# Transposing x as it lands and making h in three parts of 2, 2 and 4 k tiles

## The chip, the cores and the metric

The kernel runs on one core of a Trainium2 chip. The metric is the device time of one execution in microseconds; the time before is the median of three runs.

PE is TensorE, DVE is VectorE, ACT is ScalarE, POOL is GpSimd, SP is SyncE, which here only issues DMAs.

## The reference, cut to what matters

One layer of a hybrid block over 512 latent tokens and 256 context tokens with 1024 channels. The change lies wholly in its beginning, the modulated norm ahead of the input projection:

```python
mod  = split(silu(c)     @ w_mod + b_mod, 6)      # c:     one row of 1024
modc = split(silu(c_ctx) @ w_mod + b_mod, 6)      # c_ctx: the context's row
h  = rmsnorm(x,   norm1_g) * (1 + mod[1])  + mod[0]
hc = rmsnorm(ctx, norm1_g) * (1 + modc[1]) + modc[0]
u  = h  @ w_in                                    # gates, q, k, v, ... of three branches
uc = hc @ w_in
# mLSTM, differential attention and SSD on u and uc; gated sum, w_out, residual;
# second modulated norm, gated conv FFN, residual
```

`rmsnorm(x, g)` is `x * rsqrt(mean(x*x) + eps) * g`, the mean over the 1024 channels of a token.

## The kernel before

Everything is float32. Products with weights are made of float32r halves: a matrix is split into a high part (a cast on ACT) and a low part (a subtraction on DVE, every third one on POOL), and a product is high x high + high x low + low x high. h is kept with the channels on the partitions, as 8 k tiles of 128 channels: `hlat[0]`, `hlat[1]` (high and low part, 128 x 8 x 512) for the latent tokens and `hctx` (128 x 8 x 256) for the context.

**Phase 0** (lines 222 to 401) makes h. `xs` holds the 768 tokens in six tiles of 128 tokens by 1024 channels, loaded by three DMAs of two tiles each, the context first. ACT squares every tile with an accumulated sum (`ssq`); `rstd` (line 124) takes the reciprocal root on DVE by Newton steps, twelve small operations in a row, once for each pair of tiles; DVE scales the pair; PE transposes it in blocks of 128 x 128 into PSUM banks `psx`, four blocks to a bank; the banks are copied to `xT` (128 x 8 x 768), by turns on ACT and DVE.

Shift and scale come from `h_part(n)` (line 333), once for each of NS = 2 halves of the channels (4 k tiles): eight DMAs of w_mod, 512 KB each, into five buffers `wm`; for each, four matmuls of 256 columns with `scl` (silu of c and c_ctx) into four row groups of one PSUM bank; a copy to `msb`, two transposes, four additions to `MT`, one operation for `A1` = (1 + scale) * norm1_g. Then for each k tile and for latent and context tokens: ACT makes h's high part from xT, A1 and MT, DVE makes the same in float32 in place, and DVE (even k) or POOL (odd k) subtracts the two to get the low part.

`early(n)` (line 367) is the share of the first projections that a part of h can feed: the gates (`wgh`, `wgl`, prepared from `wgr`), the first key columns, and two sets of query columns, four PSUM banks of results that stay open over all parts. `run` (line 150) emits the chunks of `early(n - 1)` between those of `h_part(n)`; the last part's are emitted when its h is there. Weights of the projections come through `wpiece` (line 180): two buffers `wr`, four each of `wh` and `wl`.

SP issues all these DMAs in one queue: c, c_ctx, the two pieces of wgr, ctx, the norm rows, x, w_mod with pieces of w_in between. A scheduler sets the order of each engine's instructions when the kernel is built; each engine then works them off in that order.

Behind phase 0 stand `gate_rows` (line 500), a chain of ACT and DVE operations on the result of the gates' projection, and `m_proj(0)`, further projections, whose v tiles ACT copies out of PSUM (line 645).

## Time and profile before

| | us |
|---|---|
| median of three runs | 1130.47 |
| lowest, highest | 1129.69, 1135.66 |
| the profiled execution: its span | 1133.3 |
| PE busy in the span | 1088.3 (96%) |
| DVE busy | 721.9 (64%) |
| ACT busy | 477.6 (42%) |
| POOL busy | 285.3 (25%) |

Of the profiled execution only the span is given, from its first instruction to its last; it is 2.8 us longer than the median and lies between the lowest and the highest run. PE counts as busy also where its matmuls run at the lower clock or follow each other closely, so a busy PE is not PE at its peak. Of the other engines only the time matters in which PE waits for them. A row of a timeline gives the start, the duration, the engine, the line, the operation, what it writes and reads, the count and, in brackets, the idle time before it and what ended it. `PEclk` is the granted clock: 1.00 is 2.4 GHz, 0.50 is 1.2 GHz.

### The profile page before, as it was taken

The numbers are of one execution on the slowest core, as the hardware profiler recorded it, in microseconds if no ns is written. First come the engines' busy times: TensorE is split into PE (matmuls) and PEld (weight loads), VectorE is DVE, ScalarE is ACT, GpSimd is POOL, SyncE is SP. The second block draws the span as 40 slices with busy tenths as digits, with TensorE's granted clock in tenths as the row PEclk, the third lists the DMA queues.
The fourth block names the chain that finished last, engine by engine and source line by source line (L and its number), as shares of the span: only waits on it lengthen the run. The fifth ranks groups of instructions, "written<-read, shape, count | busy, mean of one in ns | idle before, by whom it ended". The sixth has DMA issues, their size and how long they took to land.

```text
span 1133.3 us, 16687 instructions
## 1 busy us (share of the span) xinstructions
PE 1088.3 (96%) x6438; PEld 949.7 (84%) x6438; DVE 721.9 (64%) x1354; ACT 477.6 (42%) x891; POOL 285.3 (25%) x243
## 2 busy tenths in 40 slices
PE   4998999999999998999999999988999999999998
PEld 3597999988888997889998887988888888888887
DVE  6578677768645568886685567677867656651211
ACT  5455454557324233334654573333543443431110
POOL 3230001026423533551061002243212212111110
PEclk9898999999999998999999999999999999999999
DMA  8621212223334337331113202425533333333421
GB/s 297 232 59 56 71 40 57 57 70 94 112 109 117 119 108 230 91 109 54 38 38 81 74 33 79 144 63 159 152 112 93 93 100 91 107 93 93 130 93 38
DMA packets 136416, 113.00 MB, mean 100 GB/s; under 512 B 6609, under 2 KB 115512, under 8 KB 136336
## 3 DMA queue, kind: packets, MB, share of 16 engines
q1 hardware_dynamic: 135712, 111.59, 32.8%
q8 instruction: 51, 0.84, 0.3%
q0 software_dynamic: 624, 0.33, 0.2%
q14 instruction: 29, 0.24, 0.1%
HBM read 109.81 MB, written 2.10 MB: 99 GB/s over the span
## 4 chain that ended last, share of the span: by engine, by line
PE 80%; DVE 9%; DMA 3%; issue 3%; ACT 3%; POOL 2%; SPq 0%; DVEq 0%; ACTq 0%; POOLq 0%
PE pl L82 56%; PE psx L82 19%; DVE t L85 2%; PE sc L82 2%; DMA wr<-in_w_in_dram 1%; ACT t L104 1%; DVE wl L85 1%; DVE t L88 1%; DMA wm<-in_w_mod_dram 1%; PE pl L949 1%; POOL t L85 1%; ACT wh L176 1%; POOL wl L85 1%; DMA t<-in_w_mod_dram 0%; PE psx L276 0%
## 5 line engine op out<-in xcount | busy, mean ns | idle before, releaser
L85 POOL TENSOR_TENSOR wl<-wr,wh 128x1024 fp32r<-128x1024 f32 x59 | 144.5, 2450 | 629.9 <-ACT wh L176 563.4
L176 ACT CAST wh<-wr 128x1024 fp32r<-128x1024 f32 x150 | 157.9, 1053 | 292.9 <-PE pl L82 179.5
L82 PE MATMUL pl<-h,wh 128*128 128x512 f32 (+1 forms) x768 | 223.2, 375 | 4.5 <-DVE ft L88 3.0
L85 DVE TENSOR_TENSOR wl<-wr,wh 128x1024 fp32r<-128x1024 f32 x91 | 119.2, 1312 | 146.8 <-ACT wh L176 144.6
L82 PE MATMUL pl<-hl,wh 128*128 128x512 f32 x608 | 200.4, 397 | 0.6 <-ACT t L758 0.4
L82 PEld LDWEIGHTS pl<-h,wh 128*128 128x128 f32 x768 | 141.0, 189 | 31.0 <-issue 4.1
L82 PE MATMUL pl<-wh,hl 128*128 128x256 f32 x768 | 151.7, 291 | 3.2 <-ACT t L645 3.2
L82 PE MATMUL pl<-h,wl 128*128 128x512 f32 (+1 forms) x384 | 143.0, 374 | 0.0
L82 PEld LDWEIGHTS pl<-hl,wh 128*128 128x128 f32 x608 | 113.0, 189 | 24.5 <-issue 2.0
L82 PEld LDWEIGHTS pl<-wh,hl 128*128 128x128 f32 x768 | 125.2, 196 | 4.1 <-ACT t L645 3.4
L82 PE MATMUL pl<-hl,wl 128*128 128x512 f32 x304 | 120.7, 397 | 0.0
L82 PE MATMUL pl<-wl,hl 128*128 128x256 f32 x384 | 111.3, 290 | 0.0
L82 PEld LDWEIGHTS pl<-h,wl 128*128 128x128 f32 x384 | 72.6, 189 | 12.8
L82 PEld LDWEIGHTS pl<-wl,hl 128*128 128x128 f32 x384 | 75.2, 196 | 0.5
L88 DVE SCALAR_TENSOR_TENSOR ft<-pl,PT,ft 128x511 f32<-128x511 f32 x88 | 65.2, 744 | 6.1 <-ACT ft L104 4.8
L82 PEld LDWEIGHTS pl<-hl,wl 128*128 128x128 f32 x304 | 57.3, 188 | 11.4
L82 PE MATMUL psx<-wl,ah 128*128 128x512 f32 (+1 forms) x176 | 66.2, 376 | 0.0
L82 PE MATMUL psx<-wh,al 128*128 128x512 f32 (+1 forms) x176 | 66.1, 376 | 0.0
L82 PE MATMUL psx<-wh,ah 128*128 128x512 f32 (+1 forms) x176 | 66.0, 376 | 0.0
L85 DVE TENSOR_TENSOR al<-ft,ah 128x512 fp32r<-128x512 f32 x22 | 45.4, 2063 | 31.0 <-ACT ah L176 31.0
L82 PE MATMUL pl<-y,wh 128*128 128x512 f32 x192 | 61.8, 402 | 0.4 <-ACT y L104 0.3
L104 ACT ACTIVATE t<-t 128x512 f32<-128x512 f32 (+4 forms) x55 | 36.9, 684 | 35.7 <-DVE t L88 34.2
(315 smaller groups left out, 2032.2 us busy)
## 6 DMA issues: line engine op xcount, KB each, us to landing
wr<-in_w_in_dram SPq DMA_DIRECT2D x64, 512.0 KB, 4.1
wr<-in_w_up_dram SPq DMA_DIRECT2D x44, 512.0 KB, 3.8
t<-in_w_mod_dram SPq DMA_DIRECT2D x48, 256.0 KB, 4.3
wr<-in_w_down_dram SPq DMA_DIRECT2D x22, 512.0 KB, 3.7
wm<-in_w_mod_dram SPq DMA_DIRECT2D x16, 512.0 KB, 8.1
wr<-in_w_out_dram SPq DMA_DIRECT2D x8, 512.0 KB, 3.4
fc<-in_w_mod_dram SPq DMA_DIRECT2D x16, 256.0 KB, 3.0
xs<-in_x_dram SPq DMA_DIRECT2D x2, 1024.0 KB
```

The lines of the kernel that those rows point to most:

```text
L82: return PE.matmul(o, l, r, start=start, stop=stop)
L85: eng.tensor_tensor(out=o, in0=x, in1=y, op=op)
L88: V.scalar_tensor_tensor(out=o, in0=x, scalar=sc, in1=y, op0=op0, op1=op1)
L104: return S.activation(o, x, f, **kw)
L176: S.copy(hi, src)
L949: PE.transpose(out=tp[:, t * P:(t + 1) * P], in_=p0[:, (t0 + t) * P:(t0 + t + 1) * P], identity=ident)
```

## The change

- x is no longer scaled ahead of the transposes: a tile is transposed as it is when it has landed. All twelve copies of `psx` to `xT` are DVE's.
- One `rstd` for all six tiles, behind them. The six columns of reciprocal roots are spread over the channels: `dg` = identity times the root, 128 x 768, and a product of ones with it (two matmuls, 512 and 256 columns) leaves each token's root on all partitions in two PSUM banks `rsp`; ACT copies them to `rsb`.
- h is made from three steps per k tile and token set: DVE xT = xT * A1 * root (the root from PSUM in the first part, from `rsb` later), ACT high part = xT + shift, DVE low part = (xT + shift) - high part. POOL does none of it.
- The parts of the channels are 2, 2 and 4 k tiles. A part of 2 loads eight pieces of 256 KB, two to a buffer, and multiplies them two by two; 16 matmuls instead of 32, and one addition more for shift and scale each.
- wgr is loaded behind x.

```diff
-    NS, NE, EX = 2, 3, 3
+    PARTS = ((0, 2), (2, 4), (4, 8))
+    NE, EX = 3, 3
...
-        nc.sync.dma_start(wgr[:, :, 0:16], wv[:, :, C_GM:C_GM + 16])
-        nc.sync.dma_start(wgr[:, :, 16:32], wv[:, :, C_DT:C_DT + 16])
         xs = p0.tile([P, 6, D], F32, name="xs")
...
+        nc.sync.dma_start(wgr[:, :, 0:16], wv[:, :, C_GM:C_GM + 16])
+        nc.sync.dma_start(wgr[:, :, 16:32], wv[:, :, C_DT:C_DT + 16])
...
-            rstd(rs[:, 2 * i:2 * i + 2], ssq[:, 2 * i:2 * i + 2], 2, 1.0 / D)
-            for t in (2 * i, 2 * i + 1):
-                ts(V, xs[:, t, :], xs[:, t, :], rs[:, t:t + 1])
...
-                if k % 4:
-                    V.tensor_copy(o, tp.rearrange("p (k c) -> p k c", k=2))
-                else:
-                    S.copy(o, tp.rearrange("p (k c) -> p k c", k=2))
+                V.tensor_copy(xT[:, k:k + 2, i * 256:(i + 1) * 256], tp.rearrange("p (k c) -> p k c", k=2))
+        rstd(rs, ssq, 6, 1.0 / D)
+        dg = p0.tile([P, 6, P], F32, name="dg")
+        tt(V, dg, ident.unsqueeze(1).broadcast_to([P, 6, P]), rs.unsqueeze(2).broadcast_to([P, 6, P]), ALU.mult)
+        rsp = [pss(), pss()]
+        mm(rsp[0], ones.broadcast_to([P, P]), dg[:, 2:6, :].rearrange("p t c -> p (t c)"))
+        mm(rsp[1][:, 0:TC], ones.broadcast_to([P, P]), dg[:, 0:2, :].rearrange("p t c -> p (t c)"))
+        rsb = p0.tile([P, NT], F32, name="rsb")
+        S.copy(rsb[:, TC:NT], rsp[0])
+        S.copy(rsb[:, 0:TC], rsp[1][:, 0:TC])
...
+                if kw == 4 or k % 2 == 0:
+                    r = p0.tile([P, 1024], F32, tag="wm", name="wm", bufs=5)
...
+                    rv = r.rearrange("p (e s c) -> p e s c", e=2, s=2)
+                    last[0] = nc.sync.dma_start(rv[:, k % 2], wsrc)
+                    if k % 2:
+                        for q in range(4):
+                            last[1] = mm(ps[32 * q:32 * q + 32, 0:256], scl[:, k - 1 + q // 2, :], rv[:, q // 2, q % 2, :],
+                                         k == 1, k == NK - 1)
...
                 for r, cs, h_ in ((0, slice(TC, NT), hlat), (1, slice(0, TC), hctx)):
-                    hins[0] = act(h_[0][:, k, :], xT[:, k, cs], AF.Identity, scale=A1[:, k, r:r + 1], bias=MT[:, 0, k, r:r + 1])
-                    ts(V, xT[:, k, cs], xT[:, k, cs], A1[:, k, r:r + 1], MT[:, 0, k, r:r + 1], ALU.mult, ALU.add)
-                    tt(G if k % 2 else V, h_[1][:, k, :], xT[:, k, cs], h_[0][:, k, :].bitcast(F32), ALU.subtract)
+                    rb = rsb[:, cs] if n else rsp[r][:, 0:cs.stop - cs.start]
+                    stt(xT[:, k, cs], xT[:, k, cs], A1[:, k, r:r + 1], rb, ALU.mult, ALU.mult)
+                    hins[0] = act(h_[0][:, k, :], xT[:, k, cs], AF.Identity, bias=MT[:, 0, k, r:r + 1])
+                    stt(h_[1][:, k, :], xT[:, k, cs], MT[:, 0, k, r:r + 1], h_[0][:, k, :].bitcast(F32), ALU.add, ALU.subtract)
```

How the order moves on the engines is shown at three places. PE at the start, before (`crow` holds the rows of c and of the norms, `xs` x, `wm` w_mod, `msb` the copied sums):

```order
L259 MATMUL psx<-ident,crow 128x32
L276 MATMUL psx<-ident,xs 128x128 x16
L82 MATMUL pl_292<-wm,scl 32x256 x12
L276 MATMUL psx<-ident,xs 128x128 x16
L82 MATMUL pl_292<-wm,scl 32x256 x8
L276 MATMUL psx<-ident,xs 128x128 x3
L82 MATMUL pl_292<-wm,scl 32x256 x4
L276 MATMUL psx<-ident,xs 128x128 x13
L82 MATMUL pl_292<-wm,scl 32x256 x4
L325 MATMUL psx<-ident,prm 128x128
L82 MATMUL pl_292<-wm,scl 32x256 x4
L351 MATMUL psx<-ident,msb 128x128 x2
```

and now:

```order
L260 MATMUL psx<-ident,crow 128x32
L275 MATMUL psx<-ident,xs 128x128 x44
L82 MATMUL pl_269<-wm,scl 32x256 x2
L275 MATMUL psx<-ident,xs 128x128 x4
L82 MATMUL pl_269<-wm,scl 32x256 x14
L82 MATMUL psx<-dg,ones 128x512
L82 MATMUL psx<-dg,ones 128x256
L329 MATMUL psx<-ident,prm 128x128
L367 MATMUL psx<-ident,msb 128x128 x2
L82 MATMUL psx<-wm,scl 32x256 x14
L82 MATMUL pl_332<-hl_104,wgh 128x512
```

The transposes stand together ahead of nearly all modulation matmuls; the two matmuls with `dg` stand between the first part's sums and their transposes, and 14 of the second part's matmuls ahead of the first one with h.

DVE at the last part of h, before (`hl_104`, `hl_105` are the high and low part of the latent h, `hct` the context's, `A_88` is A1):

```order
L85 TENSOR_TENSOR MT<-psx,PT 128x2x2 x4
L88 SCALAR_TENSOR_TENSOR A_88<-MT,NG 128x8
L94 TENSOR_SCALAR xT<-xT,A_88,MT 128x512
L94 TENSOR_SCALAR xT<-xT,A_88,MT 128x256
L85 TENSOR_TENSOR hl_105<-xT,hl_104 128x512
L85 TENSOR_TENSOR hct<-xT,hct 128x256
```

and now:

```order
L85 TENSOR_TENSOR MT<-psx,PT 128x2x2 x4
L330 COPY PT<-psx 128x128
L88 SCALAR_TENSOR_TENSOR A_88<-MT,NG 128x8
L88 SCALAR_TENSOR_TENSOR xT<-xT,A_88,rsb 128x512
L88 SCALAR_TENSOR_TENSOR xT<-xT,A_88,rsb 128x256
L88 SCALAR_TENSOR_TENSOR xT<-xT,A_88,rsb 128x512
L88 SCALAR_TENSOR_TENSOR xT<-xT,A_88,rsb 128x256
L88 SCALAR_TENSOR_TENSOR xT<-xT,A_88,rsb 128x512
L88 SCALAR_TENSOR_TENSOR xT<-xT,A_88,rsb 128x256
L88 SCALAR_TENSOR_TENSOR xT<-xT,A_88,rsb 128x512
L88 SCALAR_TENSOR_TENSOR xT<-xT,A_88,rsb 128x256
L330 COPY PT<-psx 128x128
```

The first low part (`hl_105`) stood fifth; now it stands behind the eight products and two copies of PT. On PE, ahead of that part's first h, stood twelve matmuls of the fourth projection behind the transposes of `msb`; now the two transposes of `prm` stand there alone.

ACT behind phase 0, before (`wh<-wr` is the high part of a weight piece, `t` with `psx` or `pl` a convolution's first pass or a gate row):

```order
L176 CAST wh<-wr 128x1024
L104 ACTIVATE t_666<-psx,PT 128x512
L104 ACTIVATE t_676<-t_676 64x768
L104 ACTIVATE t_698<-psx,PT 128x512
L176 CAST wh<-wr 128x1024
L104 ACT_TABLE_LOAD
L104 ACTIVATE t_688<-t_686 64x768
L104 ACT_TABLE_LOAD
L104 ACTIVATE t_686<-t_688 64x768
L176 CAST wh<-wr 128x1024
L645 COPY t_662<-pl_803 128x128
```

and now:

```order
L104 ACTIVATE t_672<-t_672 64x768
L176 CAST wh<-wr 128x1024
L104 ACTIVATE t_662<-psx,PT 128x512
L104 ACTIVATE t_694<-psx,PT 128x512
L104 ACT_TABLE_LOAD
L104 ACTIVATE t_684<-t_682 64x768
L176 CAST wh<-wr 128x1024
L104 ACT_TABLE_LOAD
L104 ACTIVATE t_682<-t_684 64x768
L176 CAST wh<-wr 128x1024
L666 COPY t_658<-pl_799 128x128
```

A cast that stood ahead of the first of the two table loads now stands between them.

## Rows read from the trace of the kernel before

**Rows 1.** Timeline of PE: start us, duration us, operation; in brackets idle before, releaser.
```profile
8.64 0.28 PE L259 MATMUL psx<-ident,crow 32*128 32x32 f32 x1 [8.64 <-DMA crow<-in_norm_g_dram]
15.04 3.67 PE L276 MATMUL psx<-ident,xs 128*128 128x128 f32 x16 [6.12 <-DVE xs L92]
...
20.63 1.97 PE L276 MATMUL psx<-ident,xs 128*128 128x128 f32 x16
...
31.51 1.08 PE L82 MATMUL psx<-wm,scl 128*32 128x256 f32 x8 [2.62 <-DMA wm<-in_w_mod_dram]
...
54.87 0.48 PE L82 MATMUL pl<-hl,wgh 128*128 128x512 f32 x1
...
68.60 0.39 PE L82 MATMUL psx<-hl,wl 128*128 128x512 f32 x1
...
89.21 0.58 PE L82 MATMUL pl<-wh,hl 128*128 128x256 f32 x1 [3.17 <-ACT t L645]
```

**Rows 2.** Stretches: from:to, length; each engine's busy us (count); PEclk, DMA share, GB/s.
```profile
2.60:5.00 2.40, 0.00 (x0) 0.00 (x0) 0.93 (x7) 0.00 (x0) 2.39 (x7) 1.00 0.98 116
6.00:19.00 13.00, 4.24 (x21) 3.65 (x25) 7.68 (x34) 10.22 (x17) 3.85 (x8) 1.00 1.03 402
30.00:37.00 7.00, 5.49 (x30) 1.98 (x30) 7.00 (x12) 5.80 (x9) 2.38 (x2) 0.51 1.07 385
88.00:95.00 7.00, 5.79 (x27) 5.79 (x28) 6.65 (x9) 1.75 (x8) 0.00 (x0) 0.51 0.01 2
596.00:601.00 5.00, 5.00 (x27) 4.81 (x28) 4.90 (x21) 3.03 (x6) 0.00 (x0) 0.66 0.00 0
756.80:764.00 7.20, 5.71 (x45) 5.50 (x46) 7.10 (x11) 3.03 (x7) 7.09 (x5) 1.00 0.26 73
```

**Rows 3.** Timeline of ACT behind the first projections.
```profile
64.60 1.05 ACT L104 ACTIVATE t<-pl,gcol 64x512 f32<-64x512 f32 x2 [5.40 <-PE pl L82]
...
73.69 1.06 ACT L176 CAST wh<-wr 128x1024 fp32r<-128x1024 f32 x1 [1.27 <-DMA wr<-in_w_in_dram]
74.77 1.28 ACT L104 ACT_TABLE_LOAD   x1
76.06 0.84 ACT L104 ACTIVATE t<-t 64x768 f32<-64x768 f32 x1
...
78.22 0.84 ACT L104 ACTIVATE t<-t 64x768 f32<-64x768 f32 x1
```

**Rows 4.** DVE's groups by form: shapes, count, busy us, mean ns, idle before.
```profile
L85 DVE TENSOR_TENSOR wgl<-wg,wgh 128x1024 fp32r<-128x1024 f32 x1 | 1.2, 1225 | 1.1 <-ACT wgh L176 1.1
L94 DVE TENSOR_SCALAR xT<-xT,A,MT 128x512 f32<-128x512 f32 x8 | 4.3, 539 | 0.9 <-ACT hl L104 0.9
L280 DVE COPY xT<-psx 128x512 f32<-128x512 f32 x6 | 4.1, 690 | 1.2 <-PE psx L276 1.0
L88 DVE SCALAR_TENSOR_TENSOR y<-psx,PT,y 128x512 fp32r<-128x512 f32 x8 | 5.8, 747 | 9.1 <-ACT y L104 9.1
L88 DVE SCALAR_TENSOR_TENSOR fc<-fc,scl 128x512 f32<-128x512 f32 x16 | 15.4, 964 | 5.3 <-DMA fc<-in_b_mod_dram 3.0 <-DMA fc<-in_w_mod_dram 2.2
L85 DVE TENSOR_TENSOR t<-t,t 64x768 f32<-64x768 f32 x4 | 3.7, 951 | 1.6 <-ACT t L104 1.5
L85 DVE TENSOR_TENSOR rs<-rs,rs 128x2 f32<-128x2 f32 x18 | 2.9, 160 | 0.5
```

**Rows 5.** PE's groups by form: the product of ones with a float32 row block.
```profile
L82 PE MATMUL psx<-fc,ones 128*128 128x512 f32 x4 | 2.0, 592 | 0.0
```

**Rows 6.** ACT's groups by form: the high part of h.
```profile
L104 ACT ACTIVATE hl<-xT,MT,A 128x512 fp32r<-128x512 f32 x8 | 6.5, 806 | 1.2 <-DVE A L88 1.2
```

**Rows 7.** Timeline of PE: two later waits.
```profile
595.93 0.89 PE L905 MATMUL pl<-identr,t 128*128 128x128 f32 x8 [2.19 <-DVE t L85]
...
758.02 0.51 PE L82 MATMUL pl<-h,wh 128*128 128x256 f32 x2 [1.23 <-DVE t L94]
```

**Rows 8.** Timeline of DVE in the gate rows.
```profile
109.27 0.56 DVE L591 COPY t<-psx 128x384 f32<-128x384 f32 x1 [3.53 <-PE psx L82]
```

More of the change, by code (lines that the diff above doesn't have):

```diff
@@ L216, in proj_w @@
         return pre.pop(c0) if c0 in pre else proj_cm(wcol(c0), lat, ctxt)
-    NS, NE, EX = 2, 3, 3
-    W = D // NS
-    KW, QW = W // P, W // 256
+    PARTS = ((0, 2), (2, 4), (4, 8))
+    NE, EX = 3, 3
     xp = es.enter_context(pool("xp", 1))
@@ L333, in h_part @@
         def h_part(n):
+            k0, k1 = PARTS[n]
+            kw = k1 - k0
+            cs_ = slice(k0 * P, k1 * P)
             ps = pss() if n else psl()
             for k in range(NK):
-                r = p0.tile([P, 2, W], F32, tag="wm", name="wm", bufs=20 // QW // 2)
-                last[0] = nc.sync.dma_start(r, a["w_mod"][0, k * P:(k + 1) * P, 0:2 * D]
-                                            .rearrange("p (s c) -> p s c", s=2)[:, :, n * W:(n + 1) * W])
-                for q in range(2 * QW):
-                    last[1] = mm(ps[32 * q:32 * q + 32, 0:256], scl[:, k, :],
-                                 r[:, q // QW, (q % QW) * 256:(q % QW + 1) * 256], k == 0, k == NK - 1)
+                if kw == 4 or k % 2 == 0:
+                    r = p0.tile([P, 1024], F32, tag="wm", name="wm", bufs=5)
+                wsrc = a["w_mod"][0, k * P:(k + 1) * P, 0:2 * D].rearrange("p (s c) -> p s c", s=2)[:, :, cs_]
+                if kw == 4:
+                    rv = r.rearrange("p (q c) -> p q c", c=256)
+                    last[0] = nc.sync.dma_start(r.rearrange("p (s c) -> p s c", s=2), wsrc)
+                    for q in range(4):
+                        last[1] = mm(ps[32 * q:32 * q + 32, 0:256], scl[:, k, :], rv[:, q, :], k == 0, k == NK - 1)
+                else:
+                    rv = r.rearrange("p (e s c) -> p e s c", e=2, s=2)
+                    last[0] = nc.sync.dma_start(rv[:, k % 2], wsrc)
+                    if k % 2:
+                        for q in range(4):
+                            last[1] = mm(ps[32 * q:32 * q + 32, 0:256], scl[:, k - 1 + q // 2, :], rv[:, q // 2, q % 2, :],
+                                         k == 1, k == NK - 1)
                 yield
@@ L345, in h_part @@
                 pt(0)
-            R = 64 * QW
             m = p0.tile([P, 256], F32, tag="xw", name="msb", bufs=3)
-            S.copy(m[0:R], ps[0:R, 0:256])
+            S.copy(m, ps[:, 0:256])
             tp = pss()
             for c in range(2):
-                PE.transpose(out=tp[:, c * P:c * P + R], in_=m[0:R, c * P:(c + 1) * P], identity=ident[0:R, 0:R])
-            ks = slice(n * KW, (n + 1) * KW)
+                PE.transpose(out=tp[:, c * P:(c + 1) * P], in_=m[:, c * P:(c + 1) * P], identity=ident)
@@ L353, in h_part @@
+            ks = slice(k0, k1)
+            tv = tp[:, 0:256].rearrange("p (c q r) -> p q c r", c=2, r=32)
             for s in (1, 0):
-                for c in range(2):
-                    tt(V, MT[:, s, ks].rearrange("p (q c) r -> p q c r", c=2)[:, :, c, :],
-                       tp[:, c * P:c * P + R].rearrange("p (q r) -> p q r", r=32)[:, s * QW:(s + 1) * QW, 0:2],
-                       PT[:, 0, s * 8 + n * KW:s * 8 + (n + 1) * KW].rearrange("p (q c) -> p q c", c=2)[:, :, c:c + 1]
-                       .broadcast_to([P, QW, 2]), ALU.add)
@@ L359, in h_part @@
-            stt(A1[:, ks], MT[:, 1, ks], 1.0, NG[:, ks].unsqueeze(2).broadcast_to([P, KW, 2]), ALU.add, ALU.mult)
-            for k in range(n * KW, (n + 1) * KW):
+                bm = PT[:, 0, s * 8 + k0:s * 8 + k1]
+                if kw == 4:
+                    for c in range(2):
+                        tt(V, MT[:, s, ks].rearrange("p (q c) r -> p q c r", c=2)[:, :, c, :], tv[:, 2 * s:2 * s + 2, c, 0:2],
+                           bm.rearrange("p (q c) -> p q c", c=2)[:, :, c:c + 1].broadcast_to([P, 2, 2]), ALU.add)
+                else:
+                    tt(V, MT[:, s, ks], tv[:, s, :, 0:2], bm.unsqueeze(2).broadcast_to([P, 2, 2]), ALU.add)
+                    tt(V, MT[:, s, ks], tv[:, 2 + s, :, 0:2], MT[:, s, ks], ALU.add)
@@ L376, in early @@
                     e[2] = (psl if e[4] else pss)() if e[5] else None
-                for k in range(n * KW, (n + 1) * KW):
-                    with tc.issue_after(last[1].ins) if n < NS - 1 else ExitStack():
+                for k in range(*PARTS[n]):
+                    with tc.issue_after(last[1].ins) if n < len(PARTS) - 1 else ExitStack():
                         proj_part(e[0], e[1], e[2], range(k, k + 1))
@@ L388, in build @@
                 e[0] = wcol(e[3])
-        for n in range(1, NS):
-            run(h_part(n), NK + EX, early(n - 1), KW * (NE + 1))
-        run(early(NS - 1))
+        for n in range(1, len(PARTS)):
+            run(h_part(n), NK + EX, early(n - 1), (PARTS[n - 1][1] - PARTS[n - 1][0]) * (NE + 1))
+        run(early(len(PARTS) - 1))
         with tc.issue_after(last[1].ins):
```

3 lines of the change are left out of this document (2 added, 1 removed).

## The prediction

> **What bounds the kernel now.** I read the timeline of PE (TensorE) first, for where it stands still: it is busy in nearly all of the span, so a change can only give back an idle stretch, work done at the lower clock, or work itself. In the stretch that the change touches PE does almost nothing until 15.04 us, when the transposes of x begin after waiting 6.12 us for VectorE's scaled x; it then works with gaps until 31.51, where it has waited 2.62 us for a w_mod piece, and from there it is busy without a break to 68.99, the end of the first projections [rows 1, 2]. So two points matter: when the unbroken run begins (31.5 now), and what it takes (37.5 us). Next come the stretches by granted clock: 30 to 37 us ran at a mean of 0.51, the 1.2 GHz level, although PE was busy 5.5 us of it; that cost about 2.7 us [rows 2]. The third view is PE's next wait: at 89.21, 20.2 us after the run's end, it has stood 3.17 us for ScalarE's copies of the v tiles, and the clock of 88 to 95 is again 0.51 with PE busy 5.79 us, another 2.9 us [rows 1, 2]. These copies stand on ScalarE behind the gate rows' chain, which starts when the gates' projection is done (64.60) [rows 3].
>
> **The start of the run.** The chain by which h becomes ready is rebuilt.
> - wgr now goes behind x. Its small pieces held the queues from 2.6 to 5.0 us at 116 GB/s [rows 2], so ctx and the c and norm rows behind it land some 2 us earlier (between 1 and 2.4): PE starts at about 6.6, not 8.64 [rows 1].
> - 48 transposes follow the landings. The first 16 took 3.67 us and later ones 1.97 [rows 1], but all twelve evictions are now VectorE's: 12 x 0.69 = 8.3 us [rows 4]. With the first bank at 7.9 and half a us of wg copies between, they end near 17.
> - Behind them in VectorE's queue: wgl 1.23; one rstd of 12 operations at 0.16 each and some 0.04 between, 2.3; the diagonal product of 768 columns at 0.95 [rows 4]. That makes 21.7. Until then nothing is gained over the old order, in which the first x was scaled at 15; what is gained is that only small work is left.
> - Spreading the root: the nearest row is another f32 product with ones, 128x512, two passes of 0.592 [rows 5], so about 1.5 us for 768 columns, or 3.0 at half clock. Three transposes of prm and msb, at 0.12 to 0.23 each [rows 1] with their hand-overs, are put at 0.6 to 0.9; the PT copy, a quarter of an eviction and a fixed part, at 0.3; five small operations on MT and A1, at rstd's rate, at 0.9.
> - Then three products (k 0 lat, k 0 ctx, k 1 lat). A scalar_tensor_tensor of 512 columns with a PSUM operand takes 0.747 [rows 4]; with 256 about 0.4: 1.9 us. Only then is the PSUM bank of the spread root free, in which part 1's modulation sums are to stand, and these are next in PE's order.
> Sum: 26.9 at full clock, 28.7 at half clock. I take 27.5: PE is busy only in pieces from 17 on and idles before the diagonal product, as it did before the drop at 30. w_mod's first part does not set this: 3.2 MB of x and wgr and 2.1 MB of w_mod, at 402 GB/s [rows 2] behind wgr's 2.4 us, are in by 19. That cover is 2.5 us.
>
> **The run itself.** PE's work from there is that of before less 16 of the 64 modulation matmuls, which now fall before it (8 took 1.08 us at half clock, so about 1.3 us at full): 37.5 - 1.3 = 36.2, with the same slow start. Two waits come new, both at the last part. Before, leftover work of the third and fourth projection hid the time from the modulation's transposes to the first h; now all of it is emitted ahead. From the transposes it takes 0.75 (MT, A1, and a PT copy that stands between), 0.75 (product) and 0.81 (ScalarE's h) [rows 4, 6]: PE waits 2.2 us, with the two PT transposes under it. Then VectorE makes all eight products before the first low part: 4 x 1.1 = 4.4, a PT copy 0.3, the low part 0.75. PE has six matmuls (1.15 us) to do in that time and next a low part: it waits another 2.4 us. After that one k tile feeds 3.5 us of PE (four of them ran from 54.87 to 68.99 [rows 1]) for 1.1 of VectorE, so VectorE is no bound any more. Such gaps cost clock too: after a wait of 2.19 us, 596 to 601 ran at 0.66, some 1.7 us; after one of 1.23, the next 7 us stayed at 1.00 [rows 2, 7]. After 3.17 it cost 2.9. I take 2.0, with 0 and 3.4 as ends. ScalarE gives up a scaled pass and GpSimd its eight low parts; neither bounds. The tensor_scalar (0.539) and the tensor_tensor of each tile become two two-tensor operations at 0.747 [rows 4]; that is in the sums.
> End of the first projections: 27.5 + 36.2 + 2.2 + 2.4 + 2.0 = 70.3, against 69.0: **+1.3 us**.
>
> **What follows.** In the new order the gates' projection is finished 32 matmuls, 6.5 us, ahead of that end (before 4.4), and on ScalarE the first table load stands right behind the last convolution's pass instead of behind a cast that waited for weights until 73.69 [rows 3]. From the end: that pass 2.2, load 1.28, Ln 0.84; the cast, whose weights are there by +4, ends at +5.4, the second load at +6.7. Exp began at 78.22, which is +9.2 [rows 3]. So the chain to the v copies comes 2.5 us earlier against the end, and the wait of 3.17 shrinks to some 0.7: **-2.5**. By the 1.23 us row the clock then holds: **-2.9**. VectorE's later part of the chain moves by 1.3 - 2.5 = -1.2 only, while PE moves by -4.1; but at 109.27 VectorE stood 3.53 us waiting for PE [rows 8], so the 2.9 between them still fit.
> Table loads: the row of 74.77 lasts 1.28 and the next operation begins at 76.06, at once [rows 3]. The Trainium skill (ScalarE: Activation LUTs, What ACT_TABLE_LOAD costs) gives 1283 ns plus about 1380 ns of drain for each switch. By the page Exp would begin at +9.4, the wait would stay, and the time would be that of the third rival; by the row it does not.
> Sum: 1.3 - 2.5 - 2.9 = -4.1 us. The profiled execution, 1133.3, would be 1129.2; it lies 2.8 above the median of the three runs, 1130.47 (1129.69 to 1135.66), of which the difference is taken: **1126.4**.
>
> **Rivals.**
> - Forecast, 0.40: 1126.4, alone between 1123 and 1130.
> - The transposes that begin at 6.6 keep PE at full clock: the run begins at 26.9 and does not lose the 2.7 us of the slow start. 1126.4 - 0.6 - 2.7 = 1123, and with a cheaper second drop 1121.5. For it: PE is busy most of 6.6 to 17. Against: the idle stretch before the diagonal product, and that all other gaps above 2 us ended at half clock. 0.25.
> - The wait at 86 doesn't close, because the gate chain hangs on something that comes as late as before (the weights' landing, GpSimd's split beside VectorE's long operation); the change then gives nothing after the head: 1130.5 + 1.3 = 1131.8. 0.26.
> - Slower: VectorE's in-order queue becomes the bound of h. Where GpSimd or DMA worked beside it, the same operation from SBUF took a mean of 0.964 [rows 4]. At that price the start comes 0.6 later, part 1's products open a wait of 1.2, the second wait at the last part grows by 1.5, and the clock costs 3.4: +4.7 on the head. The gate chain's own operations are late too and the wait at 86 stays: 1130.5 + 6.0 = 1136.5. It decides from about 0.9 per product on; against it stands that GpSimd has almost nothing left there. 0.09.
>
> **How the numbers follow.** A measurement of this kernel can tell about 0.5%, 5.65 us. Below 1124.8 lie most of the second case (0.22) and the lower tail of the forecast (0.09): faster 0.31. Above 1136.1 lies half of the last and a tail: 0.06. Within: 0.63. The range runs from the second rival's end, 1121.5, to past the third, 1133; 0.08 of the chance lies above, about as much below.
>
> **What would show it.** In the new profile: the first transpose near 6.6; the diagonal product near 21.7; the unbroken run from 27 to 28.7; two waits of 2 to 2.5 us on ScalarE and VectorE between 47 and 56, with a lower clock behind them; the end of the first projections near 70; the wait for the v copies under 1.4 us and clock 1.00 after it. If the last part's waits are missing or the run begins before 26, I was too pessimistic; if w_mod is still waited for, the smaller pieces (256 KB) land worse than reckoned; if the wait for the v copies is still 3 us, the second half of the sum falls.

## The result and the profile after

The changed kernel takes 1136.3 us (median of 20 runs, 1133.58 to 1140.9), the kernel before 1131.43 in the runs beside it (20 runs, 1124.8 to 1135.66): a ratio of 1.0053, 95% interval 1.0040 to 1.0066. It is slower by 5 to 6 us, about the 0.5% that a measurement can tell; 1126.4 was forecast, with 1121.5 to 1133 as the range. The profiled executions span 1133.3 before and 1138.0 after. Both are long ones of their kernel: before took 1135.66 in its profiled execution, the longest of its 20, and after 1139.96, against medians of 1131.43 and 1136.3.

PE's timeline after, which answers to [rows 1]: start, duration, operation, in brackets idle before and releaser.

```profile
7.56 7.82 PE L275 MATMUL psx<-ident,xs 128*128 128x128 f32 x44
...
20.12 1.98 PE L82 MATMUL pl<-wm,scl 128*32 128x256 f32 x12 [0.46 <-DMA wm<-in_w_mod_dram]
22.32 1.53 PE L82 MATMUL psx<-dg,ones 128*128 128x512 f32 x4 [0.22 <-DVE dg L85]
...
25.72 1.06 PE L82 MATMUL psx<-wm,scl 128*32 128x256 f32 x12 [1.55 <-DVE PT L330]
27.48 1.26 PE L82 MATMUL psx<-wm,scl 128*32 128x256 f32 x8 [0.70 <-DMA wm<-in_w_mod_dram]
30.06 1.64 PE L82 MATMUL psx<-wm,scl 128*32 128x256 f32 x8 [1.32 <-DMA wm<-in_w_mod_dram]
...
56.02 0.50 PE L82 MATMUL pl<-hl,wgh 128*128 128x512 f32 x1 [1.46 <-ACT hl L104]
...
59.69 0.79 PE L82 MATMUL pl<-hl,wgh 128*128 128x512 f32 x1 [2.25 <-DVE hl L88]
...
74.48 0.39 PE L82 MATMUL psx<-hl,wl 128*128 128x512 f32 x1
...
92.76 0.39 PE L82 MATMUL pl<-wh,hl 128*128 128x256 f32 x1 [0.79 <-ACT t L666]
...
100.64 0.39 PE L82 MATMUL pl<-wh,hl 128*128 128x256 f32 x1 [1.87 <-DVE t L88]
```

Stretches of the same execution, which answer to [rows 2]; the number after the five engines is the granted clock.

```profile
30.00:37.00 7.00, 6.94 (x31) 4.37 (x32) 2.32 (x4) 1.79 (x4) 0.31 (x1) 0.76 1.09 379
57.00:65.00 8.00, 5.75 (x17) 4.41 (x17) 6.68 (x19) 4.03 (x8) 0.75 (x3) 0.57 0.00 0
88.00:95.00 7.00, 6.21 (x52) 6.01 (x51) 5.13 (x9) 4.01 (x8) 0.00 (x0) 1.00 0.28 76
102.00:106.00 4.00, 4.00 (x19) 3.83 (x19) 3.94 (x10) 2.03 (x3) 0.00 (x0) 0.57 0.00 0
```

Where the time went, from these rows: the run begins at 30.06, not 31.51, but the first projections end at 74.87 (74.48 + 0.39) instead of 68.99: **+5.9**. The wait for the v copies is down from 3.17 to 0.79 (-2.4), so the matmul behind it comes at 92.76 instead of 89.21 (+3.55), and 88 to 95 runs at full clock, where before it ran at 0.51 (-2.8). Eight us on, at 100.64, PE waits 1.87 us for VectorE, and 102 to 106 runs at 0.57 (1.7 us): that gain is given back. Behind it the offset grows once more, by 1.4 us between 135 and 295, and falls by 1.8 to the end (1.2 of it at one place: PE's wait at 449 is 4.07 instead of 4.50 us, and 0.8 us less is lost to the clock behind it; in second profiles this wait is 2.65 after and 4.51 before, so its size differs from one execution to the next).

The offset is read at ScalarE's casts of the weights, the same one in both kernels. The table has it beside three starts on PE (the first matmul on h; the end of the first projections; the product that spreads the decays, `psx<-t,on`) for all kernels of this study. Offsets are against the profile of before read for the prediction, whose casts start at 134.88 and 295.29. "Later order" is explained at the low-part kernels; "other" means that it isn't before's, and is not one order for all: of these kernels only wgr first has the changed kernel's own. "4, 4, both edits" has no number at 135, since its order differs ahead of that cast (132.90).

| kernel | first h | end of first projections | decays | at 135 | at 295 | later order | span | time against before |
|---|---|---|---|---|---|---|---|---|
| before | 32.52 | 68.99 | 108.32 | 0 | 0 | before's | 1133.3 | 1 |
| before, again | 29.94 | 67.14 | 105.28 | -3.04 | -3.05 | before's | 1129.4 | |
| after | 31.62 | 74.87 | 111.40 | +5.15 | +6.50 | other | 1138.0 | 1.0053 (1.0040 to 1.0066) |
| after, again | 31.72 | 74.65 | 111.36 | +5.18 | +6.39 | other | 1137.4 | |
| wgr first | 27.73 | 72.89 | 109.32 | +3.12 | +4.49 | other | 1137.5 | 1.0072 (1.0049 to 1.0095) |
| low parts between | 30.46 | 69.64 | 108.32 | +0.07 | +1.40 | other | 1133.3 | 1.0042 (1.0023 to 1.0061) |
| the same, k-1 | 31.65 | 69.67 | 107.89 | -0.42 | -0.42 | before's | 1133.0 | 1.0021 (1.0002 to 1.0041) |
| rows of 2 KB | 29.03 | 79.51 | 116.11 | +9.90 | +11.25 | a third | 1142.8 | 1.0119 (1.0095 to 1.0143) |
| both edits | 27.31 | 68.58 | 107.97 | -0.35 | -0.39 | before's | 1130.8 | 1.0007 (0.9986 to 1.0027) |
| parts 4, 4 | 32.42 | 68.42 | 107.72 | -0.60 | -0.65 | before's | 1130.2 | 1.0002 (0.9982 to 1.0021) |
| parts alone | 30.67 | 68.77 | 108.86 | -0.26 | +1.90 | other | 1131.1 | 1.0031 (1.0011 to 1.0050) |
| 4, 4, both edits | 30.36 | 67.02 | 110.45 | | +2.87 | other | 1133.8 | 1.0049 (1.0029 to 1.0069) |
| 4, 4, wgr first | 30.32 | 69.96 | 107.95 | -0.37 | -0.38 | before's | 1129.4 | 1.0014 (0.9991 to 1.0036) |
| the same, last low part | 30.10 | 69.37 | 109.15 | +0.83 | +0.79 | before's | 1133.1 | 1.0011 (0.9991 to 1.0031) |

### The profile page after: what moved, and what is told of

It reads as the page before. It is cut to its first block, busy times and chain, and to the rows that moved or that the text cites. A ratio compares the mean times of both kernels' runs of the same rounds, so it can differ in the third digit from the quotient of the medians.

```text
span 1138.0 us, 16696 instructions
## 1 busy us (share of the span) xinstructions
PE 1094.4 (96%) x6444; PEld 952.8 (84%) x6444; DVE 720.1 (63%) x1344; ACT 472.6 (42%) x888; POOL 273.0 (24%) x235
## 4 chain that ended last, share of the span: by engine, by line
PE 78%; DVE 10%; ACT 3%; DMA 3%; SPq 2%; issue 2%; POOL 1%; DVEq 0%; ACTq 0%; POOLq 0%
PE pl L82 56%; PE psx L82 19%; PE sc L82 2%; DVE t L85 1%; DVE t L88 1%; ACT t L104 1%; DVE wl L85 1%; SPq L355 1%; DMA t<-in_w_mod_dram 1%; PE pl L970 1%; ACT wh L176 1%; DVE t L561 1%; DMA wm<-in_w_mod_dram 1%; POOL t L85 0%; SPq L256 0%
## 5 line engine op out<-in xcount | busy, mean ns | idle before, releaser
L82 PEld LDWEIGHTS pl<-h,wh 128*128 128x128 f32 x768 | 140.9, 189 | 31.5 <-issue 4.5
```

What stands on the lines that cost most here:

```text
L82: return PE.matmul(o, l, r, start=start, stop=stop)
```

## The experiments

**The same kernels again.** One profile is one execution, so both were profiled a second time.

> The changed kernel as it is, a second profile of it. Theory A (the trace's waits are fixed by the order of instructions): the waits of 0.70 and 1.32 us for w_mod before 30.06, of 1.46, 2.25 at the last part and of 1.87 at 98.77 come back within 0.3 us, and so do the stretches of lower clock. Theory B (w_mod's landing and the clock differ from run to run): the waits ahead of 30 differ by 1 to 2 us, as they did in the low-part run, which up to there has the same instructions (27.94 instead of 30.06), and the run's end differs by as much; the waits of the last part stay.

```profile
30.08 1.28 PE L82 MATMUL psx<-wm,scl 128*32 128x256 f32 x6 [1.53 <-DMA wm<-in_w_mod_dram]
...
59.61 0.79 PE L82 MATMUL pl<-hl,wgh 128*128 128x512 f32 x1 [2.25 <-DVE hl L88]
...
100.67 0.39 PE L82 MATMUL pl<-wh,hl 128*128 128x256 f32 x1 [1.86 <-DVE t L88]
```

PE's waits of the changed kernel (above, its second profile) come back within some 0.3 us as far as 110 us, and so do its stretches of lower clock: theory A, for two executions; its 20 times spread over 7.3 us. The kernel before is another matter.

> The kernel before as it is, a second profile. Theory A (waits and clock are fixed by the order of instructions, as the second profile of the changed kernel showed): the run begins at 31.2 to 31.8, 30 to 37 and 88 to 95 lose 2.5 to 3 us of clock each again, the first projections end at 68.7 to 69.3, the wait for the v copies is 3.0 to 3.3. Theory B (the profile read for the prediction was an unusual execution, since its time, 1135.66, is the highest of its runs): one of the two slow stretches is missing, the first projections end 2 us earlier or the v copies' wait is followed by the full clock.

PE's timeline in the second profile of before, and the two stretches in it that answer to 30 to 37 and 88 to 95:

```profile
31.61 0.64 PE L82 MATMUL psx<-wm,scl 128*32 128x256 f32 x8 [0.79 <-DMA wm<-in_w_mod_dram]
...
87.30 0.58 PE L82 MATMUL pl<-wh,hl 128*128 128x256 f32 x1 [3.11 <-ACT t L645]
```

```profile
29.00:36.00 7.00, 5.91 (x33) 2.83 (x34) 6.98 (x12) 5.95 (x9) 2.37 (x2) 0.76 1.07 382
86.00:93.00 7.00, 5.70 (x36) 5.70 (x37) 6.65 (x9) 2.02 (x8) 0.00 (x0) 0.76 0.01 2
```

Here w_mod's piece is waited for 0.79 us instead of 2.62 [rows 1], and the two stretches run at 0.76 instead of 0.51: 1.4 us of clock lost in each by this reckoning (5.91 x 0.24 and 5.70 x 0.24), 1.5 to 1.7 if only the time at the lower level is taken, where the prediction read 2.7 and 2.9. The first projections end 1.85 us earlier, the execution 3.9. Theory B, in a milder form: neither stretch is missing, both are shorter. The execution that the prediction rests on lies at the long end of this kernel's spread (1135.66 in 1124.8 to 1135.66), and a part of what it wanted to win back was not there in another.

**wgr back in front of ctx and x.**

```
         wgr = wgp.tile([P, NK, 32], F32, name="wgr")
+        nc.sync.dma_start(wgr[:, :, 0:16], wv[:, :, C_GM:C_GM + 16])
+        nc.sync.dma_start(wgr[:, :, 16:32], wv[:, :, C_DT:C_DT + 16])
         xs = p0.tile([P, 6, D], F32, name="xs")
...
-        nc.sync.dma_start(wgr[:, :, 0:16], wv[:, :, C_GM:C_GM + 16])
-        nc.sync.dma_start(wgr[:, :, 16:32], wv[:, :, C_DT:C_DT + 16])
```

> The changed kernel with its two wgr transfers put back ahead of ctx and x, nothing else. Theory A (bytes): the transfers ahead of the first matmuls are the same in either order, x and w_mod end when their sum has been moved, so only x lands some 2 us later and w_mod's first part still ends near 22; the unbroken run of PE begins at 30 as in the changed kernel (30.06), the first projections end between 74 and 75.5, the time stays at 1.005 of the kernel before. Theory B (blocked queue): the second wgr issue behind x holds SP's queue 5.21 us (4.22 to 9.43) and DMA falls to 83 and 108 GB/s at 12 to 14 us; without that the w_mod and w_in pieces land 2.5 to 4 us earlier, the run begins at 26 to 27.5, the first projections end at 71 to 72.5, the ratio is 1.002 to 1.003.

SP's queue in the changed kernel (start and duration of each issue, count):

```profile
3.67 0.51 SPq L255 DMA_DIRECT2D wgr<-in_w_in_dram  x1
4.22 5.21 SPq L256 DMA_DIRECT2D wgr<-in_w_in_dram  x1
9.47 6.98 SPq L355 DMA_DIRECT2D wm<-in_w_mod_dram  x8
```

The last seven of these eight, with the window begun at 12.87:

```profile
12.89 3.57 SPq L355 DMA_DIRECT2D wm<-in_w_mod_dram  x7
```

Stretches of the changed kernel (last number: GB/s), the same two with wgr first, and the second with parts of 4 and 4 (below), where wgr is behind x and the pieces are 512 KB in rows of 2 KB:

```profile
12.00:14.00 2.00, 2.00 (x14) 2.00 (x13) 1.77 (x4) 1.55 (x3) 0.33 (x1) 1.00 0.65 96
15.00:19.00 4.00, 3.33 (x24) 1.14 (x22) 4.00 (x12) 1.69 (x3) 0.00 (x0) 1.00 0.95 277
```

```profile
12.00:14.00 2.00, 1.93 (x11) 1.53 (x10) 1.76 (x4) 1.96 (x5) 0.13 (x1) 1.00 1.03 392
15.00:19.00 4.00, 4.00 (x36) 2.52 (x39) 4.00 (x9) 2.91 (x6) 0.00 (x0) 1.00 1.09 376
```

```profile
15.00:19.00 4.00, 1.99 (x24) 0.77 (x28) 3.96 (x11) 1.36 (x3) 0.00 (x0) 1.00 1.04 396
```

PE with wgr first:

```profile
25.38 2.42 PE L82 MATMUL psx<-wm,scl 128*32 128x256 f32 x20
27.73 0.50 PE L82 MATMUL pl<-hl,wgh 128*128 128x512 f32 x1
...
38.61 0.44 PE L366 MATMUL psx<-ident,msb 128*128 128x128 f32 x2 [2.80 <-ACT msb L363]
```

For the head theory B was right, but for its end: behind x the second wgr issue holds SP for 5.21 us and the first w_mod piece for another 3.4, and the queue runs dry (96 GB/s at 12 to 14; 172 in the second profile). Then SP gives out the other seven pieces in 3.57 us, 0.51 us for each 256 KB, which is faster than they move: 277 GB/s at 15 to 19. So the hold explains the dip, and not the low rate behind it. With wgr first the same pieces flow at 376, the first matmul on h comes 3.9 us earlier, and no wait for w_mod stands ahead of it. Behind the same kind of hold (4.89 us) the pieces of the 4-4 kernel moved at 396, so the size of the pieces or the length of their rows has a part as well; why small pieces are slow behind the hold and not with wgr first stays open. The gain is not kept: PE stops at 35.81 for 2.80 us, since the copy of the second part's sums stands on ScalarE behind a weight cast whose piece is late,

```profile
37.24 1.04 ACT L176 CAST wh<-wr 128x1024 fp32r<-128x1024 f32 x1 [3.09 <-DMA wr<-in_w_in_dram]
38.19 0.36 ACT L363 COPY msb<-psx 128x256 f32<-128x256 f32 x1
```

and the first projections end only 2.0 us earlier. The times do not follow (1.0072). Its interval and the changed kernel's overlap. The trace ends only 0.5 us ahead of the changed kernel's, whose profiled execution is a long one (1139.96 with a median of 1136.3), while this one is near its median; why the 2.0 us of the head don't show in the times stays open.

**Rows of 2 KB for the first two parts.** One stream of 512 KB pieces serves the sums of both parts, the h of which stay apart; the first w_in split is put behind the first h. In the second part, which the lines here don't show, a product waits for the low part of two k tiles before.

```
-                    rv = r.rearrange("p (e s c) -> p e s c", e=2, s=2)
-                    last[0] = nc.sync.dma_start(rv[:, k % 2], wsrc)
+                rv = r.rearrange("p (q c) -> p q c", c=256)
+                last[0] = nc.sync.dma_start(r.rearrange("p (s c) -> p s c", s=2), wsrc)
+                for q in range(4):
+                    o = 32 * (2 * (k % 2) + q // 2)
+                    last[1] = mm(pm[q % 2][o:o + 32, 0:256], scl[:, k, :], rv[:, q, :], k < 2, k >= NK - 2)
...
-        with tc.issue_after(last[0].ins):
+        with tc.issue_after(last[0].ins), tc.issue_after(hins[0].ins), tc.issue_after(lows[-1].ins):
```

> The changed kernel, with the modulation sums of the first two parts made together from one stream of w_mod pieces of 512 KB in rows of 2 KB (the third part as it is), so that the second part's sums no longer stand in PE's way behind the first h; the first w_in split stands behind the first h's operations on VectorE and ScalarE. The parts of h stay 2, 2 and 4. Theory A (1 KB rows): DMA moves about 400 GB/s between 14 and 24 instead of 266 to 287, both parts' sums end by 26, h begins near 28, the run begins near 28.7 without the waits of 0.70 and 1.32 for w_mod and with 12 fewer passes in it: first projections at 71.5 to 73, 1.5 to 3 us off the changed kernel's time. Theory B (row length does not matter, the rate is set by what runs beside it): the sums end at 28 or later, the run begins at 31 or later, the time is that of the changed kernel or more.

```profile
37.42 0.50 PE L82 MATMUL psx<-hl,wl 128*128 128x512 f32 x1 [2.17 <-POOL wl L85]
...
42.97 0.74 PE L82 MATMUL psx<-hl,wh 128*128 128x512 f32 x2 [1.75 <-ACT wh L176]
```

ScalarE made the first h at 28.25 and the run began at 29.03, as theory A had it, but PE then waited for the w_in pieces that now come behind all of w_mod (its timeline above): 1.0119. The pieces moved at 390 GB/s at 15 to 19 though SP's queue was held for 4.28 us ahead of them, some 400 as theory A had it, against 277 in the changed kernel: with wgr behind x, larger pieces with longer rows do help. With wgr first the small ones moved at 376, so their size alone is not the limit either.

**Low parts between the products.** In the last part the product of k tile k is put behind the low part of k-2; a second kernel, run later, has k-1 (`lows[-2]`).

```
+                    with tc.issue_after(lows[-4].ins) if k > PARTS[-1][0] + 1 and len(lows) > 3 else ExitStack():
-                    stt(xT[:, k, cs], xT[:, k, cs], A1[:, k, r:r + 1], rb, ALU.mult, ALU.mult)
+                        stt(xT[:, k, cs], xT[:, k, cs], A1[:, k, r:r + 1], rb, ALU.mult, ALU.mult)
...
+                    lows.append(stt(h_[1][:, k, :], ...))
```

> The changed kernel, in whose last part VectorE is made to do the low part of k tile k-2 before the product of tile k, instead of all eight products first. If the order of VectorE there costs what the trace says, PE's wait of 2.25 us for the first low part shrinks to under 0.5 and the half-clock stretch of 57.9 to 64.7 becomes shorter by most of its 2.5 us: the first projections end at 70 to 72.5 instead of 74.87. Theory A (the head decides the time): the whole gain stays, -2.5 to -4.7 us against the changed kernel, a ratio of 1.001 to 1.003. Theory B (given back later): the wait at 98.77 for the convolution behind the long scans grows by as much as PE is earlier, because VectorE's chain of gate rows does not come sooner; then under 1 us stays and the ratio is 1.0045 to 1.0055.

> The kernel of the low-part edit with one number changed: the product of tile k waits in VectorE's order for the low part of tile k-1 instead of k-2. The head's instructions are nearly the same, but as built the instructions that run between some 120 and 300 us then stand in the order of the kernel before, where the low-part kernel has that of the changed kernel (PE differs from before in 28 places, the last near instruction 290, instead of 127 up to instruction 1690). Theory A (the later order has a price): the end of the first projections at 69 to 71, as there (69.64), the offset to the kernel before is the same at 135 and at 295 us (before: no growth, the low-part kernel grew by 1.5), and the ratio is 1.000 to 1.002 instead of 1.0042. Theory B (the later order does not matter): the offset at 295 grows by 1 us or more again or shrinks in both, and the ratio is 1.003 to 1.005.

PE in the last part with k-2, then with k-1:

```profile
53.91 0.79 PE L82 MATMUL pl<-hl,wgh 128*128 128x512 f32 x1 [1.47 <-ACT hl L104]
...
56.21 0.63 PE L82 MATMUL pl<-hl,wgh 128*128 128x512 f32 x1
```

```profile
55.10 0.50 PE L82 MATMUL pl<-hl,wgh 128*128 128x512 f32 x1 [1.47 <-ACT hl L104]
...
56.66 0.50 PE L82 MATMUL pl<-hl,wgh 128*128 128x512 f32 x1
```

The wait of 2.25 us is gone in both (0.00 and 0.1). From its first h to its end the last part takes 18.85 us in the changed kernel (56.02 to 74.87), 15.73 with k-2, 14.57 with k-1 (55.10 to 69.67): the order cost 3.1 to 4.3 us, 2.25 of it the wait and the rest mostly the clock. Nothing of it is given back by 135 us (+0.07 and -0.42, against +5.15): the wait for the v copies is 3.4 and 3.1 us again, at an earlier time, but the wait of 1.87 us behind it is gone.

Yet the first of the two is timed at 1.0042. The second has nearly the same head and differs in what comes later. A program sets the order of instructions on each engine when the kernel is built, and a change in the head moved that order far behind it: between some 115 and 315 us the changed kernel's instructions on PE do not stand as before's do, though its source is the same there. In the table all seven traces with before's order show the same offset at 135 and at 295, within 0.05; all five with the other order and both numbers grow by 1.2 to 2.2. One place of it in the changed kernel, with no counterpart in the trace of before:

```profile
269.93 0.70 PE L82 MATMUL psx<-xw,t 128*128 128x256 f32 x2 [1.04 <-POOL xw L85]
```

So theory A of the second text holds in the trace; the ratios, 1.0042 and 1.0021, point the same way, but the second lies just past the 1.002 that it named, and their intervals overlap.

**Both edits.** wgr first, and k-2; built, it has before's later order.

> The changed kernel with both edits: wgr ahead of ctx and x, and the low parts of the last part of h between VectorE's products. Singly, the first moved the end of the first projections from 74.87 to 72.89 and the second the last part from its first h to its end by 3.1 us (56.02 to 74.87 against 53.91 to 69.64). Theory A (the head adds up and decides): the end of the first projections comes at 69 to 70.5, the matmul that waits for the v copies at 88.5 to 90.5, the ratio to the kernel before is 0.999 to 1.003. Theory B (what the head gives, clock and waits behind it take back, as the wgr edit alone showed: 2 us earlier in the trace, yet 1.0072 in the times): the ratio is 1.004 or more although the head's end comes at 70.5 or before.

The first projections end at 68.58, 6.3 us ahead of the changed kernel and 0.4 ahead of before; the offset is -0.35 at 135 and -0.39 at 295, the ratio 1.0007. Theory A: with wgr first, the low parts between and the later order back, three things at once, the three parts and the new h neither cost nor gain more than 0.3%.

**The three parts alone, in the kernel before.**

```
-    NS, NE, EX = 2, 3, 3
+    PARTS = ((0, 2), (2, 4), (4, 8))
+    NE, EX = 3, 3
```

with h_part's modulation sums as in the changed kernel, scaling, evictions and h as before.

> The kernel before with one part of the change alone: three parts of 2, 2 and 4 k tiles; x is scaled ahead of its transposes, h is made in the old way and wgr stands first, as before. Theory A (the parts are the loss, however h is made): PE has 12 or more modulation passes more behind the first h, nothing is left to fill the last part's start, the first projections end 3 to 6 us later than before (72 to 75), the ratio is 1.003 to 1.006, as in the changed kernel. Theory B (only the parts together with the two-tensor products, all eight ahead of the first low part, lose): the old tensor_scalar and the GpSimd half of the low parts keep the last part's waits under 1.5 us in sum, the first projections end at 69 to 71, the ratio is 0.999 to 1.002.

```profile
30.67 0.50 PE L82 MATMUL pl<-hl,wgh 128*128 128x512 f32 x1 [1.40 <-ACT hl L104]
...
89.44 0.58 PE L82 MATMUL pl<-wh,hl 128*128 128x256 f32 x1 [3.63 <-ACT t L662]
```

Both theories missed: the first projections end at 68.77, better than either said, and the ratio is 1.0031. At the last part PE waits 0.83 us for h, and 0.40 at the transposes ahead of it. The loss is behind the head, -0.26 at 135 and +1.90 at 295: the other later order.

**Parts of 4 and 4 with the new h.**

```
-    PARTS = ((0, 2), (2, 4), (4, 8))
+    PARTS = ((0, 4), (4, 8))
```

> The changed kernel with two parts of 4 and 4 k tiles instead of 2, 2 and 4: x transposed as it lands, the spread root and wgr's place stay. w_mod then comes in rows of 2 KB, as before, and leftover work of the first part can be spread over the second. Theory A (the three parts are the loss): DMA runs near 400 GB/s instead of 266 to 287 at 15 to 19 us, the run begins between 29 and 31.5 but holds 64 instead of 76 passes of the modulation, there is no wait of 1.5 and 2.2 us at the last part, and the first projections end at 67 to 70.5; the ratio is 0.996 to 1.001. Theory B (the new way of making h is the loss): VectorE's products come as late and as dense in any part, the first projections end at 73 or later, the ratio is 1.004 or more.

```profile
55.44 0.50 PE L82 MATMUL pl<-hl,wgh 128*128 128x512 f32 x1 [1.43 <-DVE hl L88]
```

1.0002 (within 0.2% either way); of theory A's two bounds the ratio holds and the end, 68.42, too; the wait at the last part, which it had expected to be gone, remains with 1.43 us. The new way of making h, from an x that is transposed as it lands and scaled later, moves the time by nothing that shows when the parts stay at 4 and 4.

**Versions meant to beat both kernels.** All three have parts of 4 and 4 and wgr first (both diffs above). The first also has the low parts between the products, in both parts; the second has nothing more; the third puts the product of k tile 7 alone behind a low part. The line that the first and the third add:

```
+                    with tc.issue_after(lows[-4].ins) if k % 4 > 1 and len(lows) > 3 else ExitStack():
```

```
+                    with tc.issue_after(lows[-2].ins) if k > PARTS[-1][0] + 2 and len(lows) > 3 else ExitStack():
```

> The new way of making h (x transposed as it lands, root spread by the diagonal product) in two parts of 4 and 4, with wgr ahead of ctx and x and the low parts between the products. Theory A: from the 4-4 run's end of the first projections (68.42) the last part's wait of 1.43 us for a low part and the late start (run from 30.1 behind w_mod pieces) go: end at 64.5 to 67, the wait for the v copies grows by less than that, the ratio is 0.995 to 0.999. Theory B (DMA bounds the head: x, w_mod and the first w_in pieces must land in any order): the run begins earlier but stops for w_mod or w_in pieces in between, the end comes at 67.5 to 68.5 and the ratio is 0.999 to 1.002.

> The new way of making h in two parts of 4 and 4, wgr ahead of ctx and x, no edit of the low parts; the later instructions stand in the order of the kernel before. Theory A (the head's gain stays where the later order is that of before): against the same with wgr behind x (end of the first projections 68.42, ratio 1.0002) the w_mod issues are not held up by SP, the end comes at 66.5 to 68 and the ratio is 0.997 to 1.000. Theory B (behind the head the chain of the gate rows decides): the end comes earlier, but the product that spreads the decays stays within 0.5 us of the kernel before (108.32) and the ratio is 0.9995 to 1.002.

> As the kernel with parts of 4 and 4 and wgr first, and in the last part the product of the last k tile behind the low part of the one before; the later instructions stand in the order of the kernel before. Theory A: the wait for the first low part (1.43 us in the 4-4 run) becomes under 0.7, the end of the first projections lies 0.5 to 1.5 us ahead of the 4-4 kernel with wgr first, the ratio is 0.996 to 0.999, better than both kernels. Theory B (the chain of the gate rows decides): the end comes earlier and the wait for the v copies (2.91 us there) grows by the same, the ratio is 0.9995 to 1.002.

PE, ScalarE and VectorE in the first of them:

```profile
89.48 0.39 PE L82 MATMUL pl<-wh,hl 128*128 128x256 f32 x1 [1.67 <-ACT t L669]
...
110.45 0.91 PE L82 MATMUL psx<-t,on 64*128 64x384 f32 x2 [3.50 <-DVE t L85]
```

```profile
106.52 1.05 ACT L176 CAST wh<-wr 128x1024 fp32r<-128x1024 f32 x1 [2.31 <-DMA wr<-in_w_in_dram]
```

```profile
108.70 1.70 DVE L85 TENSOR_TENSOR t<-ident,sm 64x384 f32<-64x384 f32 x1 [3.16 <-ACT sm L104]
```

It is the best head of all: the first projections end 2.0 us ahead of before. PE then waits for v copies twice, 0.65 us to 81.79 and 1.67 to 89.48, where before stood at 89.21 after its one wait, and at the decays (110.45) it is 2.1 us behind before. The gate rows' chain did not come earlier with the head; it was even held up, since a weight cast that waits 2.31 us for its DMA stands ahead of its exponentials on ScalarE, and VectorE and PE wait behind it. The ratio is 1.0049, and neither theory had that. In the other two the runs begin earlier and stop for w_mod or for h:

```profile
33.43 1.08 PE L82 MATMUL psx<-wm,scl 128*32 128x256 f32 x8 [1.76 <-DMA wm<-in_w_mod_dram]
```

(the second kernel's PE), and the third waits 4.62 us for the v copies, more by 1.7 than the plain 4-4 kernel. 1.0014 and 1.0011: by the ratios theory B in both, though no clear difference from 1 is measured, and in the second kernel the end of the first projections, 69.96, came 1.0 later than before's. No version here beats the kernel before.

## Why the prediction was wrong

**The start** (forecast 27.5, measured 30.06). The sum on VectorE was right nearly term by term: the diagonal product ended at 22.17 (21.7), its spread took 1.53 (1.5), the products 0.75. The step that failed is that the sum ends there: it takes part 1's sums for the start of the run, and gives the second part's w_mod pieces, next in PE's order, no time at all. PE waited 0.70 and 1.32 us for them; these 2.0 and the 0.5 by which the diagonal product was late make nearly all of the 2.6 us. The pieces were late because the sum counted bytes at 402 GB/s and let wgr behind x only help: behind x it held SP's queue, and the pieces came at 277. "w_mod's first part does not set this ... That cover is 2.5 us" just held, with 0.2 us of it left: PE summed the first part until 22.10 and then waited 0.22 for VectorE. "Only then is the PSUM bank ... free" did not hold: these sums began at 25.72, released by the PT copy, ahead of the first product (26.44). "If w_mod is still waited for, the smaller pieces (256 KB) land worse than reckoned" was named as a sign of failure. That is a part of the cause: with wgr first the small pieces moved at 376, and behind x pieces of twice the size at 390 to 396. The Trainium skill (DMA: Bandwidth & Descriptors, Bandwidth) calls transfers under 64 KB descriptor-dominated. The two of wgr have exactly 64 KB and so stand at the edge of that rule, not under it; they moved at 11 to 13 us, and the rate at 12 to 14 was 96 GB/s.

**The run** (36.2 of work). A slip of bookkeeping: the modulation has 128 passes in both kernels. Before, 64 of them are behind the start; I took 16 off, but the first part now has only 32, so that 76 are left behind 30.06. PE's passes by form in the run, before (31.5 to 69.0) and after (30.05 to 74.9):

```profile
L82 PE MATMUL psx<-wm,scl 128*32 128x256 f32 x64 | 7.0, 478 | 2.6 <-DMA wm<-in_w_mod_dram 2.6
```

```profile
L82 PE MATMUL psx<-wm,scl 128*32 128x256 f32 x76 | 7.2, 408 | 1.3 <-DMA wm<-in_w_mod_dram 1.3
```

28 more than forecast, at some 0.08 us (28 in a row took 2.39 us with wgr first), are 2.2 us. **The waits at the last part** were nearly right: 0.40 + 1.46 and 2.25 against 2.2 and 2.4, which is 4.1 for 4.6, and the clock behind them lost 2.5 against 2.0. The lower clock at the run's start cost 1.7, not 2.7. Start, passes, clock at the last part, clock at the start and waits, 2.6 + 2.2 + 0.5 - 1.0 - 0.5, make 3.8 of the 4.6 us by which the end missed 70.3; the other 0.8 is not assigned. The runs with the low parts between show that the second wait with its clock, rightly forecast at 4.4 and measured at 3.1 to 4.3, was the largest single cost in the head's trace; the sum set it against gains that did not come. In the times its removal shows less: k-2 alone is at 1.0042 against 1.0053, and the intervals overlap.

**The gate chain** (-2.5): right, 0.79 against 0.7. The table loads came as the row of before had it: ScalarE after,

```profile
76.76 1.28 ACT L104 ACT_TABLE_LOAD   x1
78.05 0.85 ACT L104 ACTIVATE t<-t 64x768 f32<-64x768 f32 x1
```

with the next operation at once behind the load (76.76 + 1.28 = 78.04). The Trainium skill (ScalarE: Activation LUTs, What ACT_TABLE_LOAD costs) has about 1380 ns of drain beside the load for every switch to another set. No row here shows it, and the prediction was right to go by its row.

**The clock behind it** (-2.9): the rows came as forecast (88 to 95 at 1.00), and the time did not. The step that failed is "the 2.9 between them still fit". It looked at VectorE's wait at 109.27 [rows 8], and took for the changed kernel the banks that PE asked for in the kernel before. VectorE after:

```profile
95.83 4.24 DVE L561 TENSOR_TENSOR_SCAN t<-t,t 32x768 f32<-32x768 f32 x3
100.10 1.14 DVE L88 SCALAR_TENSOR_TENSOR t<-pl,PT,t 128x255 f32<-128x255 f32 x2
```

PE's 49th matmul from the wait for the v copies on needs the bank that these two convolution steps empty, and they stand behind three scans, 7.34 us after that wait's end. PE at full clock was there 1.87 us too early, stood still, and lost 1.7 us of clock for it. VectorE is no later than before: there the same steps come 7.34 us after the wait's end too (at 96.55 for 89.21). What differs is the bank. In the kernel before the 49th matmul (97.54) depends, by its semaphore, on a copy of ScalarE, and only the 73rd needs VectorE's bank. The second profile of before shows it, VectorE and PE:

```profile
94.64 1.14 DVE L88 SCALAR_TENSOR_TENSOR t<-pl,PT,t 128x255 f32<-128x255 f32 x2
```

```profile
94.38 0.40 PE L82 MATMUL pl<-wh,hl 128*128 128x256 f32 x2
```

PE's 49th matmul stands there at 94.50, ahead of these steps and without a wait; the 73rd came at 97.38, when the steps had long been done. With this hand-out of the banks the gain in the clock would have had room. The changed kernel as built, the one with wgr first and the one with rows of 2 KB have the other (waits of 1.87, 1.87 and 1.86 us); the kernels with low parts between and the one with the parts alone do not. No run changes the hand-out by itself.

**Not in the sum at all**: the later order (1.2 to 2.2 us in traces), and that the profile of before was a long one (by 3.0 us at 135 against its second).

**The rivals.** The slower one gave 1136.5, next to the measured 1136.3, by a mechanism that did not come: the products kept to 0.75 us. A right number for a wrong reason; its chance was too small because the costs of the head were thought known.

How the 5 to 6 us split between head and later order in the times stays open. Whatever the head, the five kernels with before's later order lie at 1.0002 to 1.0021, and the six with another at 1.0031 to 1.0119. But in the traces the order is worth 0.1 to 0.2%, less than this gap, and the kernel with the earliest end of the first projections (67.02) is at 1.0049. The times thus give the order more, and the head less, than the traces do, and no run changes the order alone. Open too is the time of the kernel with wgr first.

## What to carry to other kernels

Count moved work as a balance over the whole program, not as a difference at one place, and price every DMA that stands behind a moved one on its queue. Before a gain of clock or of a wait is booked, look in the kernel as it is built for the next bank that PE needs in that stretch, and for the engine that empties it: an edit far ahead can change both. Where a program sets the order, a change in one stage has to be looked for in all later ones, and a second profile of the kernel before shows which of its waits are there to be won.
